# Softmax attention and output projection of a hybrid block: a written order on four engines in place of a planned one

## The chip, the core and the metric

The kernel runs on one core of a Trainium2 chip. The core has a matrix engine (TensorE, PE in the profile, with its weight loads as PEld), three engines for elementwise work (VectorE = DVE, ScalarE = ACT, GpSimd = POOL) and a queue that issues transfers (SyncE = SP). [...] The metric is the device time of one launch in microseconds. Before the change it was 778.51 us, the median of three runs (777.87 to 778.65).

## The reference

One layer of a transformer block on 512 tokens of width 1024. The normed input is projected; a gated linear attention (GLA) of four heads and a softmax attention (MLA) of eight heads run on the projection; their gated sum goes through an output projection; a squared-ReLU MLP and a final norm follow. What matters here:

```python
    def attend(qblk):
        s = jnp.einsum('bhqd,bhkd->bhqk', qblk, kt).astype(jnp.float32)
        p = jax.nn.softmax(s, axis=-1)
        return jnp.einsum('bhqk,bhkv->bhqv', p.astype(vt.dtype), vt)
...
    merged = jax.nn.sigmoid(z_ma) * y_gla + jax.nn.sigmoid(z_mb) * y_mla
    h = h + merged @ w_out[l]
    m = rmsnorm(h, g_mlp[l])
    h = h + jnp.square(jax.nn.relu(m @ w_ff1[l])) @ w_ff2[l]
```

## The kernel before

**Numbers in two halves.** [...] `split` (line 92) is the pair: ACT copies the source into the high half, then DVE (or POOL, if told) subtracts the high half from the source into the low half. So a low half always waits for its high half. A product is three matmuls, `mm3` (lines 88 to 90).

**Attention.** There are 8 heads of 4 tiles of 128 queries, 32 tiles in all. The loop behind line 1243 counts n from 0 to 37. In step n it computes the scores of tile n (`att_scores`, line 1000), transposes the probabilities of tile n-3 (`att_flip`, line 1018) and, in odd steps, multiplies two tiles with the values (`att_values`, line 1029). `att_scores` is: three matmuls into a bank `s`, the row maximum on DVE (L1007), the exponential with its row sum on ACT (L1010), the reciprocal of the sum on DVE (L1011), and the scaling of the tile by it, on DVE for odd tiles (L1013) and on ACT for even ones (L1015). `att_flip` is four transposes into a bank `tp` (L1024) and a `split` of it into `pT` (ACT at L93, DVE at L94). The banks of `s` and `tp` come out of one set of four in PSUM. After the fourth tile of a head, `merge` (line 1045) multiplies the result by its gate on DVE (L1052) and adds the GLA part on POOL (L1055).

**Units.** `up_units(pr)` (line 945) is a generator for the pair of heads pr: first loads and splits of the pair's weights (high halves on ACT, low ones on POOL), then, one piece per call, the queries (two split pairs), the keys (two) and the values (two calls, one each). They are interleaved with the steps.

**Output projection.** It is computed with seven block products in place of eight: 1, 2, 5, 6, 3, 7 and 4, each of 24 matmuls for two row blocks (`wo_product`, line 1463). Its left operands are sums of blocks of the merged rows: `split_first` gives those of products 1 and 2, `split_sum` those of 5 and 6 (from y) and of 7 and 3 (from z), where `merged_sums` makes y and z. Its right operands are the four blocks B11, B12, B21, B22 of `w_out` and sums of them. A sum comes about in one of two ways: `load_onto` (line 904) has POOL issue two transfers that add a block out of memory onto a tile, and `add_w2` (line 910) adds on DVE. `split_part` splits one half of such a tile (two 128 x 512 parts) for TensorE.

**After the projection** the rows are added to the residual (`add_rows`), squared and scaled (`normed`, line 1309: a square on ACT, one operation on DVE, a power on POOL, one scaling on DVE and one on ACT), transposed (`flipped`), and the first two products of the MLP begin.

**What sets the order.** A planner orders the instructions of each engine by the program's order, by when operands and buffers come free, and by a table of costs, at the time the program is built. `in_program_order(start, engines)` (line 110) ties each instruction traced since `start` to the one before it on its engine, so that engine runs exactly as written; `goes_behind` ties one group behind another. Before the change, everything on ACT and DVE up to the third GLA head and the whole projection on PE, ACT and DVE run as written, attention on POOL alone; on PE, ACT and DVE the planner orders attention. SP is always the planner's.

Of the kernel before, what the change touches and what calls it, by code (L numbers as in the profile page):

```python
# [15 lines left out]
ALU = mybir.AluOpType  # L16
# [3 lines left out]
S = 512  # L20
# [36 lines left out]
def tile_block(ctx: ExitStack, tc: tile.TileContext, t, out: bass.AP):  # L57
# [16 lines left out]
    def sm(name, n=4, dt=F32):  # L74
        return tl([P, n], dt, "sm", 24, name)
# [31 lines left out]
    def traced():  # L107
        return len(nc.cur_bb.bb.instructions)
# [755 lines left out]
    def split_first(left, px, name, rest=nc.vector, g=None, c=slice(0, S)):  # L864

        g = u4(f"ga{name}") if g is None else g
        split(g[:, 0, c], g[:, 1, c], px[:, c], rest)
        left[1] = g[:, 0, 0:HT], g[:, 1, 0:HT]
        left[2] = g[:, 0, HT:S], g[:, 1, HT:S]
        return g  # L870

    def split_sum(left, src, m_lo, m_hi, name, rest=nc.vector):
        h, l = u2(f"gh{name}", F32R), u2(f"gl{name}", F32R)
        split(h, l, src, rest)
        left[m_lo] = h[:, 0:HT], l[:, 0:HT]
        left[m_hi] = h[:, HT:S], l[:, HT:S]
# [17 lines left out]
    def block_rows(w, qd, x, g, pp_):  # L894
        r = (qd * FQ + 2 * (2 * g + pp_) + x // 2) * P
        c = (x % 2) * S
        return w[r : r + P, c : c + S]

    def load_w2(qd, x, w=w2):
        for g, dst in enumerate(block_tiles(x)):  # L900
            for pp_ in range(2):
                nc.sync.dma_start(dst[:, pp_, :], block_rows(w, qd, x, g, pp_))

    def load_onto(dst, x, w):

# [4 lines left out]
    def add_w2(dst, x, y, op):  # L910
        for g in range(NP // 2):
            nc.vector.tensor_tensor(wq[dst][g], wq[x][g], wq[y][g], op=op)  # L912

    def split_part(x, g, name):
        wh, wl = halves(2, S, f"{name}{g}")
# [3 lines left out]
    def split_w2(x, name):  # L919
        return [split_part(x, g, name) for g in range(NP // 2)]  # L920
# [77 lines left out]
    probs, pTs, avs = {}, {}, {}  # L998

    def att_scores(head, qt):  # L1000
        q, kb, _, _ = heads[head]
        tok = slice(qt * P, (qt + 1) * P)
        acc = ps("at", f"s{head}{qt}")
        d = slice(0, NOPE + ROPE)
        mm3(acc, q[d, 0, tok], q[d, 1, tok], kb[d, 0, :], kb[d, 1, :], True, True)
        top = sm("top", 1)
        nc.vector.tensor_reduce(top, acc, axis=AX.X, op=ALU.max, negate=True)  # L1007
        e = u2(f"e{head}{qt}")
        tot = sm("tot", 1)
        nc.scalar.activation(e, acc, AF.Exp, bias=top, accum_out=tot)  # L1010
        nc.vector.reciprocal(tot, tot)  # L1011
        if qt % 2:
            nc.vector.tensor_scalar(e, e, tot, None, op0=ALU.mult)  # L1013
        else:
            nc.scalar.activation(e, e, AF.Copy, scale=tot)  # L1015
        probs[head, qt] = e

    def att_flip(head, qt):
        e = probs.pop((head, qt))
# [219 lines left out]
    rs = gla_squares(h, os)  # L1239
    gla_gated(h, os, rs)  # L1240
    LAG_B, LAG_C = 3, 6
    units = iter(())
    attending = traced()
    sums_of = {}
    for n in range(4 * MH + LAG_C):
        if n % 8 == 1 and n // 8 + 1 < MH // 2:
            units = up_units(n // 8 + 1)
        scored = traced()
        if n < 4 * MH:
            att_scores(n // 4, n % 4)  # L1250
        scored = scored, traced()
        next(units, None)
        b = n - LAG_B
        if 0 <= b < 4 * MH:
            flips = traced()
            att_flip(b // 4, b % 4)
            if b == 0:
                gla_turn(GH - 1, (flips, traced()))

        ready = traced()  # L1260
        if n in (17, 25, 31):
            p = (n - 13) // 8
            y, z = sums_of.pop(p)
            split_sum(wo_left[p], y, 5, 6, f"bo{p}", nc.gpsimd)
            split_sum(wo_left[p], z, 7, 3, f"co{p}", nc.gpsimd)
            if p == 1:
                for p in range(2):
                    split_first(wo_left[p], merged[p][0], f"o{p}", nc.gpsimd)
            goes_behind((ready, traced()), scored, SPLITTERS[:1])
        if n == 20:  # L1270
# [12 lines left out]
        if c >= 0 and c % 2 == 1:  # L1283
            att_values(c // 4, (c % 4) // 2)
        if c > 0 and c % 8 == 7 and c // 8 < NP - 1:
            sums_of[c // 8] = merged_sums(c // 8, nc.gpsimd)

    hrow = []
    for i in range(NT):
# [16 lines left out]

    span = {}

    def normed(i, last_half):
        at = traced()  # L1310
        m = ms_rows[i]
        square_half(hrow[i], last_half, hparts[i], m, False)
        rs = row_rstd(hparts[i])
        nc.vector.tensor_scalar(m[:, 0:S], hrow[i][:, 0:S], rs, None, op0=ALU.mult)
        nc.scalar.activation(m[:, S:D], hrow[i][:, S:D], AF.Copy, scale=rs)
        span["norm", i] = at, traced()

    def flipped(i):
        fm.rows(i, ms_rows[i])
# [134 lines left out]

    begun = traced()
    xs_ = [ps("at", f"wox{rb}") for rb in range(2)]
    zs_ = [ps("at", f"woz{rb}") for rb in range(2)]
    ws_ = [ps("mm", f"wow{rb}") for rb in range(2)]  # L1460
# [10 lines left out]
                    m in (1, 2, 5) and p == 0, p == NP - 1, m not in (1, 2, 5))  # L1471

    last = NP - 1
    split_first(wo_left[2], merged[2][0], "o2", nc.vector)
# [4 lines left out]
    y, z = merged_sums(last, nc.vector)  # L1479
    split_sum(wo_left[last], y, 5, 6, f"bo{last}")  # L1480
    wo_right[5].append(split_part(B11, 1, "bo5"))
    load_onto(B12, B22, w_out)
    add_w2(B11, B22, B11, ALU.add)
    for rb in range(2):
        add_rows(rb, 0, xs_[rb])
    wo_product(2)
    wo_right[6] = [split_part(B11, 0, "bo6")]
    for rb in range(2):
        add_rows(rb, 0, ws_[rb])
        first_half_square(rb, 0)  # L1490
    wo_right[6].append(split_part(B11, 1, "bo6"))
    load_onto(B11, B21, w_out)
    load_w2(0, B21)
    split_sum(wo_left[last], z, 7, 3, f"co{last}")
    wo_product(5)
    wo_right[3] = [split_part(B22, 0, "bo3")]
    for rb in range(2):
# [20 lines left out]
    for rb in range(2):  # L1518
        wo_product(7, (rb,))
        add_rows(2 + rb, 1, xs_[rb], ALU.subtract)  # L1520
        first_half_square(2 + rb, 1)
        flipped(rb)
    early.append(proj_begin(w1, P, "f01", "at"))
    for rb in range(2):
        wo_product(4, (rb,))
        add_rows(2 + rb, 0, xs_[rb])
        normed(2 + rb, 0)
    proj_run(early[0], mT, 0)
    proj_run(early[1], mT, 0, range(5))
    flipped(2)  # L1530
# [80 lines left out]
```

## Time and profile before

| | us |
|---|---|
| median of three runs | 778.51 |
| the profiled execution | 777.01 |
| its span, first to last instruction | 775.3 |
| TensorE busy | 757.8 |
| VectorE busy | 584.6 |
| ScalarE busy | 452.9 |
| GpSimd busy | 148.9 |
| first scores of attention begin | 303.73 |
| first product of the projection begins | 388.0 |

A row of a view begins with its start in us where it is a timeline, then the length, the engine, the line of the kernel, the operation and what it writes from what. In brackets is the idle time of the engine just before it, with the instruction whose end ended that idle time. A row of groups has the number of instructions behind an x, then their busy time in us and the mean of one in ns, then the idle time ahead of them.

### The profile page before, as it was taken

The page shows a single profiled execution, that of the slowest core. Times are in us where ns is not written, and L with a number is a line of the kernel's source. Part 1 is how long each engine was busy: PE and PEld are TensorE (multiplying, and loading weights), DVE is VectorE, ACT ScalarE, POOL GpSimd, SP SyncE. Part 2 cuts the span into 40 slices and gives each one's busy share as a digit, 9 for nine tenths or more (in the row PEclk, how much of TensorE's full clock was granted, in tenths as well). Part 3 has the DMA queues.
Part 4 walks back from the last instruction along what each step waited for, and adds up shares of the span by engine and source line. Part 5 has one row for each costly group of instructions (what it writes and reads, how often), then busy time and mean ns, then how long its engine had stood idle before and what let it go on. Part 6 is the DMA issues. An engine that isn't in the chain of part 4 may idle for free.

```text
span 775.3 us, 10210 instructions
## 1 busy us (share of the span) xinstructions
PE 757.8 (98%) x3744; PEld 640.1 (83%) x3744; DVE 584.6 (75%) x866; ACT 452.9 (58%) x768; POOL 148.9 (19%) x224
## 2 busy tenths in 40 slices
PE   9999999999999999999799899999999999999996
PEld 7888788889888888898687788888888888888885
DVE  7788999666677776989887677965787578848695
ACT  7556667556475546978735675544644465336644
POOL 0810006161533124044741000000000000000014
PEclk9999999999999999999899899999999999999999
DMA  9734201132325324014766231164106510560002
GB/s 313 244 110 135 71 18 29 54 82 55 82 55 135 52 55 106 22 36 142 219 162 187 84 109 55 58 202 120 55 30 188 151 40 27 171 183 0 28 1 108
DMA packets 94945, 77.09 MB, mean 99 GB/s; under 512 B 15312, under 2 KB 74704, under 8 KB 94896
## 3 DMA queue, kind: packets, MB, share of 16 engines
q1 hardware_dynamic: 92752, 72.24, 31.6%
q0 software_dynamic: 1856, 3.93, 2.7%
q8 instruction: 29, 0.48, 0.3%
q10 hardware_dynamic: 288, 0.28, 0.1%
q14 instruction: 20, 0.16, 0.1%
HBM read 72.76 MB, written 2.10 MB: 97 GB/s over the span
## 4 chain that ended last, share of the span: by engine, by line
PE 93%; DVE 4%; issue 1%; ACT 1%; POOL 0%; POOLq 0%; DVEq 0%; ACTq 0%
PE f L89 8%; PE f L90 8%; PE f L88 8%; PE gx L88 4%; PE gx L89 4%; PE gx L90 4%; PE first L326 3%; PE za L88 2%; PE za L89 2%; PE za L90 2%; PE gz L89 2%; PE gz L90 2%; PE gz L88 2%; PE tp L1024 2%; PE zb L88 1%; PE zb L90 1%
## 5 line engine op out<-in xcount | busy, mean ns | idle before, releaser
L1550 POOL DMA_DIRECT2D gfin<-in_g_final x1 | 0.6, 622 | 283.7 <-PE f L90 283.7
L912 DVE TENSOR_TENSOR w<-w,w 128x1024 f32<-128x1024 f32 x34 | 41.1, 1220 | 0.3
L474 POOL COPY v3f<-rrf 128x4 f32<-128x4 f32 x4 | 2.8, 708 | 135.8 <-DVE rrf L457 135.8
L1010 ACT ACTIVATE e<-s,top 128x512 f32<-128x512 f32 x32 | 21.9, 685 | 6.7 <-DVE top L1007 6.1
L1298 DVE TENSOR_TENSOR h<-h,gx 128x512 f32<-128x512 f32 x32 | 21.5, 680 | 1.9 <-PE gx L90 1.8
L1007 DVE TENSOR_REDUCE top<-s 128x1 f32<-128x512 f32 x32 | 21.6, 679 | 1.4 <-PE s L90 1.4
L94 DVE TENSOR_TENSOR pT<-tp,pT 128x512 fp32r<-128x512 f32 x32 | 21.5, 679 | 0.4 <-ACT pT L93 0.2
L93 ACT ACTIVATE pT<-tp 128x512 fp32r<-128x512 f32 x32 | 18.8, 594 | 4.9 <-PE tp L1024 4.9
L88 PE MATMUL av<-pT,v 128*128 128x256 f32 x64 | 19.5, 304 | 1.3 <-ACT pT L93 1.3
L1024 PE MATMUL tp<-ident,e 128*128 128x128 f32 x128 | 20.1, 281 | 0.0
L89 PE MATMUL av<-pT,v 128*128 128x256 f32 x64 | 18.6, 291 | 0.1
L1024 PEld LDWEIGHTS tp<-ident,e 128*128 128x128 f32 x128 | 16.2, 146 | 3.1 <-issue 0.4
L1370 ACT ACTIVATE fa<-f 128x512 f32<-128x512 f32 x32 | 18.5, 577 | 0.0
L90 PE MATMUL av<-pT,v 128*128 128x256 f32 x64 | 18.4, 288 | 0.0
L93 ACT ACTIVATE ghb<-y 128x512 fp32r<-128x512 f32 x16 | 10.1, 632 | 14.0 <-DVE y L859 14.0
L94 DVE TENSOR_TENSOR sc<-sc,sc 128x512 fp32r<-128x512 f32 x16 | 10.9, 690 | 9.5 <-ACT sc L93 9.5
L88 PE MATMUL s<-kbuf,q 96*128 96x512 f32 x32 | 14.5, 453 | 3.2 <-DVE pT L94 3.2
L93 ACT ACTIVATE sc<-sc 128x512 fp32r<-128x512 f32 x16 | 9.3, 596 | 11.5 <-DVE sc L545 11.5
L1055 POOL TENSOR_TENSOR mx<-tb,za 128x256 f32<-128x256 f32 x8 | 6.9, 868 | 40.9 <-DVE tb L1052 40.9
L93 ACT ACTIVATE b_00h<-w 128x1024 fp32r<-128x1024 f32 x7 | 7.4, 1060 | 12.6 <-PE gx L90 6.0
L93 ACT ACTIVATE b_10h<-w 128x1024 fp32r<-128x1024 f32 x7 | 7.4, 1061 | 12.1 <-PE gz L90 6.0
L93 ACT ACTIVATE b_20h<-w 128x1024 fp32r<-128x1024 f32 x7 | 7.4, 1060 | 11.9 <-PE gz L90 6.0
(1639 smaller groups left out, 2940.7 us busy)
## 6 DMA issues: line engine op xcount, KB each, us to landing
w<-in_w_ff SPq DMA_DIRECT2D x64, 256.0 KB, 3.4
grw<-in_w_in SPq DMA_DIRECT2D x8, 512.0 KB, 8.6
gvw<-in_w_in SPq DMA_DIRECT2D x8, 512.0 KB, 4.8
w<-in_w_out SPq DMA_DIRECT2D x16, 256.0 KB, 5.2
w<-in_w_out POOLq DMA_DIRECT2D x6, 512.0 KB, 7.9
x<-in_xt SPq DMA_DIRECT2D x8, 256.0 KB, 5.3
vw<-in_w_first SPq DMA_DIRECT2D x8, 256.0 KB, 5.4
h<-in_x SPq DMA_DIRECT2D x4, 512.0 KB, 10.7
```

The costliest lines, as they stand in the source:

```text
L88: nc.tensor.matmul(acc, lh, rh, start=start, stop=False, skip_group_check=onto)
L89: nc.tensor.matmul(acc, lh, rl, start=False, stop=False, skip_group_check=onto)
L90: nc.tensor.matmul(acc, ll, rh, start=False, stop=stop, skip_group_check=onto)
L93: nc.scalar.activation(hi, src, AF.Copy)
L94: rest.tensor_tensor(lo, src, raw(hi), op=ALU.subtract)
L326: nc.tensor.matmul(f_accs[i], a[:, i * P : (i + 1) * P], b, start=k == 0 and x == 0, stop=k == KD - 1 and x == 2)
L912: nc.vector.tensor_tensor(wq[dst][g], wq[x][g], wq[y][g], op=op)
L1007: nc.vector.tensor_reduce(top, acc, axis=AX.X, op=ALU.max, negate=True)
L1010: nc.scalar.activation(e, acc, AF.Exp, bias=top, accum_out=tot)
L1024: nc.tensor.transpose(tp[:, k * P : (k + 1) * P], e[:, k * P : (k + 1) * P], ident)
L1298: nc.vector.tensor_tensor(hc, hc, acc, op=op)
L1370: nc.scalar.activation(a, acc, AF.Relu)
```

## The change

- All of PE, ACT, DVE and POOL run as written from the loop's begin (`attending`) to the end of the projection. The `goes_behind` calls of the loop go.
- The reciprocal and the scalings leave `att_scores`. `att_normalise`, at the begin of each even step, takes one reciprocal for tiles n-2 and n-1 together and scales the first on ACT and the second on DVE.
- The units of pair 1 begin ahead of the loop, those of pairs 2 and 3 load in steps 6 and 14; the pieces come in steps with n % 8 from 2 to 6.
- The weights of products 1 and 2 no longer pass through the tiles of B11 and B21: `streamed` loads each half into a staging buffer and splits it in steps 11, 13, 21 and 23. Tile B21 is then filled with block B22, and POOL's transfers add B11 and B12 onto it (steps 27 and 31): the weights of product 6, which DVE added before. B21 itself is added onto it for product 4.
- Sums and splits of the left operands get steps of their own; one `split_first` goes from POOL to DVE.
- In the projection `normed` is taken apart into `second_half_square` and `scaled`, the latter with both halves on ACT for the first two row blocks, and the order of the pieces around products 3, 7 and 4 is another.

```diff
-    def load_w2(qd, x, w=w2):
+    def load_w2(qd, x, w=w2, block=None):
...
+    def streamed(m, x, g):
+
+        wf = stage(2, S, f"bo{m}{g}")
+        for pp_ in range(2):
+            nc.sync.dma_start(wf[:, pp_, :], block_rows(w_out, 0, x, g, pp_))
+        wh, wl = halves(2, S, f"bo{m}{g}")
+        split(wh, wl, wf)
+        wo_right.setdefault(m, []).append((wh, wl))
...
-        tot = sm("tot", 1)
-        nc.scalar.activation(e, acc, AF.Exp, bias=top, accum_out=tot)
+        if qt % 2 == 0:
+            tots[head] = sm("tot", 2)
+        tot = tots[head]
+        nc.scalar.activation(e, acc, AF.Exp, bias=top, accum_out=tot[:, qt % 2 : qt % 2 + 1])
+        probs[head, qt] = e
+
+    def att_normalise(head, qt):
+        tot, a, b = tots[head], probs[head, qt], probs[head, qt + 1]
         nc.vector.reciprocal(tot, tot)
-        if qt % 2:
-            nc.vector.tensor_scalar(e, e, tot, None, op0=ALU.mult)
-        else:
-            nc.scalar.activation(e, e, AF.Copy, scale=tot)
-        probs[head, qt] = e
+        nc.scalar.activation(a, a, AF.Copy, scale=tot[:, 0:1])
+        nc.vector.tensor_scalar(b, b, tot[:, 1:2], None, op0=ALU.mult)
...
-    units = iter(())
+    units = up_units(1)
+    next(units)
     attending = traced()
     sums_of = {}
     for n in range(4 * MH + LAG_C):
-        if n % 8 == 1 and n // 8 + 1 < MH // 2:
-            units = up_units(n // 8 + 1)
-        scored = traced()
+        if n % 2 == 0 and 2 <= n <= 4 * MH:
+            att_normalise((n - 2) // 4, (n - 2) % 4)
         if n < 4 * MH:
             att_scores(n // 4, n % 4)
-        scored = scored, traced()
-        next(units, None)
+        if 2 <= n % 8 < 7:
+            next(units, None)
+        if n in (6, 14):
+            units = up_units(n // 8 + 2)
+            next(units)
...
-        ready = traced()
-        if n in (17, 25, 31):
...
+        for x, at in (("y", (18, 26, 32)), ("z", (20, 28, 33))):
+            if n in at:
+                p = at.index(n)
+                to = (5, 6) if x == "y" else (7, 3)
+                split_sum(wo_left[p], sums_of[p, x], *to, f"{x}o{p}", nc.gpsimd)
+        if n in (19, 30):
+            p = (19, 30).index(n)
+            split_first(wo_left[p], merged[p][0], f"o{p}", nc.gpsimd)
+        if n == 35:
+            split_first(wo_left[2], merged[2][0], "o2")
+        if n in (11, 13):
+            streamed(1, B11, (n - 11) // 2)
+        if n in (21, 23):
+            streamed(2, B21, (n - 21) // 2)
+        if n == 22:
             load_w2(0, B11, w_out)
-            load_w2(0, B21, w_out)
-        if n == 24:
-            wo_right[1] = split_w2(B11, "bo1")
+        if n == 23:
+            load_w2(0, B21, w_out, B22)
+        if n == 25:
+            load_onto(B11, B12, w_out)
         if n == 27:
-            wo_right[2] = split_w2(B21, "bo2")
+            load_onto(B21, B11, w_out)
         if n == 28:
-            load_onto(B11, B12, w_out)
-        if n == 30:
             load_w2(0, B12, w_out)
             load_w2(0, B22, w_out)
+        if n == 31:
+            load_onto(B21, B12, w_out)
+        if n == 34:
+            load_onto(B12, B22, w_out)
...
-    load_onto(B12, B22, w_out)
-    add_w2(B11, B22, B11, ALU.add)
+    load_w2(0, B11)
...
-    wo_right[6] = [split_part(B11, 0, "bo6")]
+    wo_right[6] = [split_part(B21, 0, "bo6")]
...
-        normed(rb, 1)
-        wo_right.setdefault(4, []).append(split_part(B11, rb, "bo4"))
-    load_w2(0, B11)
+        second_half_square(rb, 1)
+    wo_right[4] = [split_part(B21, 0, "bo4")]
+    for rb in range(2):
+        scaled(rb, True)
+    wo_right[4].append(split_part(B21, 1, "bo4"))
+    load_w2(0, B21)
+    wo_product(7, (0,))
+    add_rows(2, 1, xs_[0], ALU.subtract)
+    first_half_square(2, 1)
+    flipped(0)
+    wo_product(7, (1,))
+    add_rows(3, 1, xs_[1], ALU.subtract)
+    first_half_square(3, 1)
     early = [proj_begin(w1, 0, "f00", "at")]
...
-    in_program_order(begun, PE_ONLY + SPLITTERS)
-    in_program_order(attending, (mybir.EngineType.Pool,))
+    in_program_order(attending, PE_ONLY + SPLITTERS + (mybir.EngineType.Pool,))
```

More of the change, by code (lines that the diff above doesn't have):

```diff
@@ L1486, in tile_block @@
     wo_product(2)
-    wo_right[6] = [split_part(B11, 0, "bo6")]
+    wo_right[6] = [split_part(B21, 0, "bo6")]
     for rb in range(2):
         add_rows(rb, 0, ws_[rb])
+    wo_right[6].append(split_part(B21, 1, "bo6"))
+    load_onto(B21, B21, w_out)
+    split_sum(wo_left[last], z, 7, 3, f"co{last}")
+    for rb in range(2):
         first_half_square(rb, 0)
[L1491 to L1494, printed above, removed]
     wo_product(5)
@@ L1513, in tile_block @@
         add_rows(rb, 1, zs_[rb])
-        normed(rb, 1)
-        wo_right.setdefault(4, []).append(split_part(B11, rb, "bo4"))
-    load_w2(0, B11)
-    early = [proj_begin(w1, 0, "f00", "at")]
[L1518 to L1522, printed above, removed]
+        second_half_square(rb, 1)
+    wo_right[4] = [split_part(B21, 0, "bo4")]
+    for rb in range(2):
+        scaled(rb, True)
[8 more added lines that the diff above has]
+    first_half_square(3, 1)
+    early = [proj_begin(w1, 0, "f00", "at")]
+    flipped(1)
     early.append(proj_begin(w1, P, "f01", "at"))
@@ L1525, in tile_block @@
         wo_product(4, (rb,))
+        at = traced()
         add_rows(2 + rb, 0, xs_[rb])
-        normed(2 + rb, 0)
+        second_half_square(2 + rb, 0)
+        scaled(2 + rb, False)
+        span["norm", 2 + rb] = at, traced()
     proj_run(early[0], mT, 0)
```

29 lines of the change are left out of this document (10 added, 19 removed).

## The prediction

> **What bounds the kernel now.** I read the page first, then the busy times of the engines in three stretches: the attention loop up to its last weight loads, its end, and the output projection.
>
> ```profile
> PE 757.8 (98%) x3744; PEld 640.1 (83%) x3744; DVE 584.6 (75%) x866; ACT 452.9 (58%) x768; POOL 148.9 (19%) x224
> 303.73:359.00 55.27, 55.27 (x367) 49.67 (x366) 49.44 (x101) 46.10 (x104) 15.52 (x21) 1.00 0.27 77
> 359.00:388.00 29.00, 24.45 (x154) 21.49 (x153) 26.26 (x45) 22.42 (x47) 21.33 (x21) 0.88 0.51 150
> 388.00:445.00 57.00, 52.62 (x268) 44.23 (x267) 40.92 (x64) 29.39 (x54) 13.12 (x18) 0.94 0.56 146
> ```
>
> The columns of a stretch are its length, then the busy time of PE, PEld, DVE, ACT and POOL, the granted clock, and two of DMA. TensorE is busy in 98% of the span, and in the first 55 us of attention without a gap. There is something to win only where it is not: 29.00 - 24.45 = 4.6 us in the end of attention and 57.00 - 52.62 = 4.4 us in the projection. The order in time on TensorE shows where, and two short stretches show what follows a gap.
>
> ```profile
> 372.51 0.38 PE L88 MATMUL av<-pT,v 128*128 128x256 f32 x1 [1.35 <-ACT pT L93]
> 375.62 0.79 PE L88 MATMUL s<-kbuf,q 96*128 96x512 f32 x1 [2.73 <-DVE pT L94]
> 430.64 0.79 PE L88 MATMUL wox<-bo40h,gdo 128*128 128x512 f32 x1 [3.08 <-DVE h L1298]
> 375.00:380.00 5.00, 4.38 (x14) 3.58 (x15) 3.60 (x8) 2.65 (x6) 5.00 (x6) 0.50 0.89 290
> 430.00:435.00 5.00, 4.36 (x10) 3.47 (x11) 3.83 (x9) 4.38 (x13) 0.37 (x2) 0.50 0.64 206
> ```
>
> After each of the two long gaps the granted clock is 0.50 in the next stretch, so about 4.4 us of work takes twice its time: another 2.2 us each. All that a perfect order of these stages could win is therefore 4.6 + 4.4 + 2.2 + 2.2 = 13.4 us.
>
> **The change, part by part.** It fixes the order of ACT, DVE, PE and POOL from the first attention step to the projection's end as it is written. In step n the writing gives, on DVE: (reciprocal and one scaling, n even), the maximum of tile n, a unit's low halves, the low half of the transposed tile n-3. On ACT: (one scaling, n even), the exponential of tile n, a unit's high halves, the high half of tile n-3. The queues take turns: the exponential waits for the maximum; the high half stands behind the exponential; the low half waits for the high half; and the next maximum stands behind the low half. That is a ring through two engines, once per step, and TensorE cannot shorten it. Its durations:
>
> ```profile
> L1007 DVE TENSOR_REDUCE top<-s 128x1 f32<-128x512 f32 x32 | 21.6, 679 | 1.4 <-PE s L90 1.4
> L94 DVE TENSOR_TENSOR pT<-tp,pT 128x512 fp32r<-128x512 f32 x29 | 19.6, 678 | 0.4 <-ACT pT L93 0.2
> L1013 DVE TENSOR_SCALAR e<-e,tot 128x512 f32<-128x512 f32 x16 | 9.9, 620 | 0.4
> L1011 DVE RECIPROCAL tot<-tot 128x1 f32<-128x1 f32 x32 | 4.9, 155 | 2.6 <-ACT e L1010 2.5
> L1052 DVE SCALAR_TENSOR_TENSOR tb<-tb,av 128x512 f32<-128x512 f32 x7 | 4.8, 680 | 1.2 <-PE av L90 1.2
> L94 DVE TENSOR_TENSOR bo10l<-w,bo10h 128x1024 fp32r<-128x1024 f32 x1 | 1.2, 1220 | 0.0
> L1010 ACT ACTIVATE e<-s,top 128x512 f32<-128x512 f32 x32 | 21.9, 685 | 6.7 <-DVE top L1007 6.1 <-DVE tot L1011 0.4
> L1015 ACT ACTIVATE e<-e,tot 128x512 f32<-128x512 f32 x16 | 11.5, 717 | 0.3 <-DVE tot L1011 0.3
> L93 ACT ACTIVATE pT<-tp 128x512 fp32r<-128x512 f32 x30 | 17.7, 593 | 4.9 <-PE tp L1024 4.9
> L93 ACT ACTIVATE bo10h<-w 128x1024 fp32r<-128x1024 f32 x1 | 1.0, 1048 | 0.0
> L93 ACT ACTIVATE wk2h<-wk2f 128x128 fp32r<-128x128 f32 (+1 forms) x4 | 1.1, 351 | 0.0
> L93 ACT ACTIVATE wq3h<-wq3f 128x384 fp32r<-128x384 f32 x1 | 0.5, 519 | 0.0
> 366.64 0.68 DVE L1007 TENSOR_REDUCE top<-s 128x1 f32<-128x512 f32 x1
> 367.35 0.69 ACT L1010 ACTIVATE e<-s,top 128x512 f32<-128x512 f32 x1 [0.25 <-DVE top L1007]
> 367.94 0.19 ACT L1010 ACTIVATION_READ_ACCUMULATOR e<-s,top 128x1 f32 x1
> 368.03 0.59 ACT L93 ACTIVATE pT<-tp 128x512 fp32r<-128x512 f32 x1
> 383.08 0.68 DVE L1007 TENSOR_REDUCE top<-s 128x1 f32<-128x512 f32 x1
> 383.68 0.68 DVE L94 TENSOR_TENSOR pT<-tp,pT 128x512 fp32r<-128x512 f32 x1
> 384.28 0.68 DVE L1007 TENSOR_REDUCE top<-s 128x1 f32<-128x512 f32 x1
> 383.01 0.60 ACT L93 ACTIVATE pT<-tp 128x512 fp32r<-128x512 f32 x1 [0.41 <-PE tp L1024]
> 383.86 0.69 ACT L1010 ACTIVATE e<-s,top 128x512 f32<-128x512 f32 x1 [0.25 <-DVE top L1007]
> ```
>
> From maximum to exponential is 367.35 - 366.64 = 0.71; from there to a high half on the same engine 368.03 - 367.35 = 0.68; the high half lasts 0.59, and a waiting engine starts about 0.03 later, as the exponential did (366.64 + 0.68 = 367.32): 0.62; on DVE one operation follows another after 0.60 (383.08, 383.68, 384.28). Sum 2.61 us a step. The rows at 383 show how the kernel before avoids it: there ACT does the high half (383.01) ahead of the exponential (383.86), so DVE goes maximum, low half, maximum in 1.2 us.
>
> That a written order really turns in such rings, the attention's predecessor shows, which already runs in written order: masked copy and low half on DVE, high half on ACT.
>
> ```profile
> 179.51 0.60 ACT L93 ACTIVATE sc<-sc 128x512 fp32r<-128x512 f32 x1 [0.96 <-DVE sc L545]
> 181.07 0.60 ACT L93 ACTIVATE sc<-sc 128x512 fp32r<-128x512 f32 x1 [0.96 <-DVE sc L545]
> 180.14 0.69 DVE L94 TENSOR_TENSOR sc<-sc,sc 128x512 fp32r<-128x512 f32 x1 [0.66 <-ACT sc L93]
> 180.74 0.29 DVE L545 COPY_PREDICATED sc<-after,bds 128x128 f32<-128x128 int32 x1
> ```
>
> One turn takes 181.07 - 179.51 = 1.56; by my rule 0.63 + 0.60 + 0.29 + 0.03 = 1.55. The ring is counted rightly to a hundredth. [...]
>
> Now the terms, for steps 3 to 31 (29 steps):
> - The ring alone: 29 x 2.61 = 75.7.
> - In the 14 even steps DVE does the shared reciprocal (0.155 + 0.03) and one scaling (0.40 at its usual pace) ahead of the maximum: 14 x 0.59 = 8.3. ACT's scaling (0.72) runs beside DVE's and the maximum and costs nothing; without that cover it is 14 x 0.6 = 8.6. Sharing the reciprocal saves 16 x 0.155 = 2.5 of DVE time, already in this.
> - Units. A low half in the ring adds 0.60 for each of v's two. For q and k two pairs read one bank, and the trace has the second high half waiting for the first low half:
>
> ```profile
> 352.61 0.68 DVE L94 TENSOR_TENSOR kbuf<-uk,kbuf 64x512 fp32r<-64x512 f32 x1
> 353.32 0.59 ACT L93 ACTIVATE kbuf<-uk 64x512 fp32r<-64x512 f32 x1 [0.51 <-DVE kbuf L94]
> ```
>
>   So 0.71 + 0.62 + 0.60 = 1.93 more each, or 1.2 if q does not wait so. In steps 3 to 31: k three times, q twice, v six times: 5 x 1.93 + 6 x 0.60 = 13.3 (9.6 at the least).
> - The next pair's weights (steps 6 and 14): ACT's high halves stand between exponential and high half, 1.1 + 0.5 less the overlap, about 1.4 each: 2.8.
> - Two gates turned (step 3) and six merges, 0.60 each on DVE: 4.8.
> - The four streamed weight parts (11, 13, 21, 23): ACT's 1.05 starts 0.48 after the high half (which follows as ACT's operations do), DVE's 1.22 behind it starts at 1.56 and frees DVE at 2.70 where it was free at 1.22: 4 x 1.5 = 5.9. At the least DVE's own 4 x 1.13 = 4.5.
>
> Sum 75.7 + 8.3 + 13.3 + 2.8 + 4.8 + 5.9 = 110.8 us.
>
> ```profile
> 306.46 1.87 DVE L1007 TENSOR_REDUCE top<-s 128x1 f32<-128x512 f32 x3
> 386.98 0.68 DVE L94 TENSOR_TENSOR pT<-tp,pT 128x512 fp32r<-128x512 f32 x1
> 400.74 2.36 DVE L912 TENSOR_TENSOR w<-w,w 128x1024 f32<-128x1024 f32 x2
> L908 POOL DMA_DIRECT2D w<-in_w_out x6 | 7.4, 1373 | 1.0 <-DVE bo61l L94 1.0
> ```
>
> The first maxima stand at 306.46 now and should after; two exponentials, the reciprocal, the third maximum and q's pairs bring the maximum of tile 3 to about 313.1, so the low half of tile 28 (step 31) ends near 313.1 + 110.8 = 423.9. Now it is at 386.98 + 0.60 = 387.6. **The loop costs +36.3 us.** The three low halves, two value products and the merges behind it are the same work as now: 0, within 2.
>
> The projection: the weight sum on DVE (2.36) goes, but DVE is not what TensorE waits for there except at 430: 0, at best -2.4 were it on the path. Two sums more by transfers are four issues more on POOL (1.37 each, 5.5 us) and eight more loads on SP; POOL is busy 21 of 29 us at the end of attention now, and with 36 us more to do it in, nothing waits for it; without that cover up to 5.5. The stall at 430 is late rows: now an addition stands behind normalising and two weight splits. After, it stands behind four ACT scalings (4 x 0.72 = 2.9) and the second part of the weights of product 4, while TensorE has one block (2.8) to do: much the same gap. I take -1; the bounds are -6.6 (gap and clock gone) and +3 (both scalings fully in the open).
>
> Against the profiled execution, 777.01 us (span 775.3 and 1.7 around it): 777.0 + 36.3 - 1 = 812.3. It lies 1.5 below the median of the runs, 778.51, so for the median **814 us**.
>
> **The rivals.**
> *The written order fits, faster.* The two gaps go and the ring does not bind, because ACT or DVE are never late: 778.5 - 13.4 = 765 at best. For it: both engines have idle time in each step (49.4 and 46.1 busy of 55.3). Against it: attention up to the last low half takes 387.6 - 306.46 = 81 us now, and the ring with nothing but its even steps takes 32 x 2.61 + 15 x 0.59 = 92. It decides from a ring under 81 / 32 = 2.5 us.
> *Only the bare ring, little slower.* Units, streams and merges slip into DVE's waiting time instead of adding to it: 92 - 81 = +11, less 1: 789. For it: DVE waits 1.4 of every 2.6 us. Against it: in the queue the additions stand behind ACT work that itself follows the exponential, past that wait.
> *The clock falls, much slower.* TensorE has 55.27 + 24.45 = 79.7 us of work, 2.2 of it an effect of the half clock, in some 121 us, with a gap in nearly every step. If those gaps held the clock at 0.50, it would need 2 x 77.5 = 155 where stage and gaps take 84 now: +71, 849. For it: the clock fell after the gaps of 4.1 and 3.1 us. Against it: gaps here are about 1 us each. [...]
> *The order isn't followed.* If the added order edges did not bind ACT and DVE, their planner would be as free as now, only the moved weights and sums would count: between 765 and 779.
>
> **How the numbers follow.** Full ring 0.76; bare ring 0.08; half clock 0.04; written order fits 0.09; order not followed 0.03. The full ring's own range: at the least 36.3 - 3.7 - 1.4 - 2 - 6.6 = +22.6, so 801; at the most DVE's scaling at twice its pace while POOL works (14 x 0.5 = 7), 3 in the projection instead of -1, 5.5 of POOL, 2 in the tail and two falls of the clock (2 x 2.2): +36.3 + 22, so 837. To leave no more than 2 in 10 out, the range goes down to the bare ring: 788 to 837. No change can be told within 0.2%, about 1.6 us. Slower: 0.76 + 0.08 + 0.04 = 0.88; of the two others 0.02 falls within 0.2%, and 0.10 is faster.
>
> **What would show it.** In the profile after: ACT's idle time ahead of the exponential put down to the maximum rises from 6.1 us to some 30; DVE's ahead of the low half, put down to ACT, from 0.2 to over 15; TensorE's busy share in the attention near 0.7; maxima 2.6 us apart in odd steps without a unit and 3.2 in even ones. I am wrong if maxima of steps 24 to 31 come at less than 2.5 us apart on average, if ACT does a high half ahead of the exponential of its step, or if the clock in attention is not near 1.

## The result, and the profile after

| | before | after |
|---|---|---|
| median of four runs, us | 778.19 (777.27 to 778.65) | 823.56 (823.01 to 824.18) |
| ratio to before, 95% interval | | 1.0585 (1.0566 to 1.0603) |
| the profiled execution, us | 777.01 | 823.11 |
| its span, us | 775.3 | 821.4 |

The change costs 45 us. The kernel before has one run more here than in the table ahead of the prediction, 777.27, so its median is 778.19 in place of 778.51. Of the page after, the busy times first:

```profile
PE 773.0 (94%) x3744; PEld 648.2 (79%) x3744; DVE 581.8 (71%) x846; ACT 457.5 (56%) x770; POOL 151.2 (18%) x228
```

DVE and ACT do as much as before (584.6 and 452.9 us); the span has grown by 46.1 us, TensorE's busy time by 15.2, with the same 3744 matmuls. So nothing was added to be done: TensorE waits, and part of its work runs slower. The busy times in three stretches of the kernel after, columns as in the prediction (length, PE, PEld, DVE, ACT, POOL, clock, DMA):

```profile
303.73:359.00 55.27, 43.84 (x234) 36.05 (x232) 33.75 (x59) 30.80 (x65) 4.93 (x8) 0.88 0.11 28
359.00:428.00 69.00, 48.16 (x267) 40.02 (x267) 41.28 (x68) 38.75 (x83) 31.42 (x37) 0.88 0.56 161
428.00:485.00 57.00, 51.80 (x258) 44.43 (x259) 35.82 (x57) 29.88 (x54) 15.89 (x19) 0.94 0.58 139
```

In the first 55 us of attention TensorE had no gap before (busy 55.27 of 55.27); now it is idle for 55.27 - 43.84 = 11.4, and for 20.8 in the next 69. No engine is full in either stretch. Who waits for whom stands in the groups of instructions of the kernel after (its L1022 is the exponential, L1017 the maximum, L1028 ACT's scaling, L1027 the shared reciprocal, L1037 the transposes):

```profile
L1037 PE MATMUL tp<-ident,e 128*128 128x128 f32 x128 | 23.8, 317 | 27.5 <-ACT e L1028 25.6
L94 DVE TENSOR_TENSOR pT<-tp,pT 128x512 fp32r<-128x512 f32 x32 | 22.0, 689 | 29.4 <-ACT pT L93 29.3
L1022 ACT ACTIVATE e<-s,top 128x512 f32<-128x512 f32 x32 | 22.0, 687 | 30.2 <-DVE top L1017 30.2
L1028 ACT ACTIVATE e<-e,tot 128x512 f32<-128x512 f32 x16 | 11.6, 722 | 20.3 <-DVE tot L1027 20.3
```

DVE waits 29.3 us for ACT's high half ahead of its low half (0.2 before), ACT waits 30.2 for DVE's maximum ahead of its exponential (6.1 before). Two engines that wait 30 us for each other, neither of them full: that is the ring. The chain of waits in order of time shows two turns of it, each piece with its start, its length and what ran:

```profile
416.93 0.60 DVE top L1017
417.56 0.78 ACT e L1022 x2
418.34 0.49 ACT pT L93
418.85 0.69 DVE pT L94
419.54 0.61 DVE top L1017
420.18 0.78 ACT e L1022 x2
420.96 0.49 ACT pT L93
421.47 0.69 DVE pT L94
```

No TensorE piece is in it. From low half to low half one turn takes 421.47 - 418.85 = 2.62 us.

### The profile page after: what moved, and what is told of

The parts are those of the page before. It is cut to its first block, busy times and chain, and to the rows that moved or that the text cites. A ratio compares the mean times of both kernels' runs of the same rounds, so it can differ in the third digit from the quotient of the medians.

```text
span 821.4 us, 10236 instructions
## 1 busy us (share of the span) xinstructions
PE 773.0 (94%) x3744; PEld 648.2 (79%) x3744; DVE 581.8 (71%) x846; ACT 457.5 (56%) x770; POOL 151.2 (18%) x228
## 4 chain that ended last, share of the span: by engine, by line
PE 79%; DVE 10%; ACT 7%; issue 2%; POOL 1%; DMA 0%; POOLq 0%; ACTq 0%; DVEq 0%
PE f L89 7%; PE f L90 7%; PE f L88 7%; PE gx L88 4%; PE gx L89 4%; PE gx L90 4%; PE first L326 3%; ACT e L1022 3%; DVE top L1017 2%; DVE pT L94 2%; PE za L88 2%; PE za L89 2%; PE za L90 2%; PE gz L89 2%; PE gz L88 2%
## 5 line engine op out<-in xcount | busy, mean ns | idle before, releaser
L1037 PE MATMUL tp<-ident,e 128*128 128x128 f32 x128 | 23.8, 317 | 27.5 <-ACT e L1028 25.6
L1037 PEld LDWEIGHTS tp<-ident,e 128*128 128x128 f32 x128 | 17.3, 162 | 36.3 <-ACT e L1028 30.7
L94 DVE TENSOR_TENSOR pT<-tp,pT 128x512 fp32r<-128x512 f32 x32 | 22.0, 689 | 29.4 <-ACT pT L93 29.3
L913 DVE TENSOR_TENSOR w<-w,w 128x1024 f32<-128x1024 f32 x32 | 38.7, 1219 | 0.3
L1022 ACT ACTIVATE e<-s,top 128x512 f32<-128x512 f32 x32 | 22.0, 687 | 30.2 <-DVE top L1017 30.2
L88 PE MATMUL av<-pT,v 128*128 128x256 f32 x64 | 23.0, 359 | 0.6 <-DVE tb L1065 0.6
L1028 ACT ACTIVATE e<-e,tot 128x512 f32<-128x512 f32 x16 | 11.6, 722 | 20.3 <-DVE tot L1027 20.3
L1017 DVE TENSOR_REDUCE top<-s 128x1 f32<-128x512 f32 x32 | 21.7, 680 | 0.0
L89 PE MATMUL av<-pT,v 128*128 128x256 f32 x64 | 21.5, 335 | 0.0
L90 PE MATMUL av<-pT,v 128*128 128x256 f32 x64 | 21.4, 335 | 0.0
L88 PEld LDWEIGHTS av<-pT,v 128*128 128x128 f32 x64 | 15.6, 244 | 0.8 <-issue 0.8
L90 PEld LDWEIGHTS av<-pT,v 128*128 128x128 f32 x64 | 15.7, 246 | 0.0
```

The costliest lines, as they stand in the source:

```text
L88: nc.tensor.matmul(acc, lh, rh, start=start, stop=False, skip_group_check=onto)
L89: nc.tensor.matmul(acc, lh, rl, start=False, stop=False, skip_group_check=onto)
L90: nc.tensor.matmul(acc, ll, rh, start=False, stop=stop, skip_group_check=onto)
L94: rest.tensor_tensor(lo, src, raw(hi), op=ALU.subtract)
L1037: nc.tensor.transpose(tp[:, k * P : (k + 1) * P], e[:, k * P : (k + 1) * P], ident)
```

## The experiments

Each "ratio" is to the kernel before, run on the same chip at the same time, with its 95% interval. Medians are of four runs.

**The exponential behind the high half.** The kernel after, with one ACT instruction elsewhere: in step n the exponential of tile n follows the high half of tile n-3. All four engines still run as written. What `att_scores` did behind the maximum becomes `att_exp`, which `att_flip` calls through `between`.

```diff
         nc.vector.tensor_reduce(top, acc, axis=AX.X, op=ALU.max, negate=True)
+        scored_[head, qt] = acc, top
+
+    def att_exp(head, qt):
+        acc, top = scored_.pop((head, qt))
         e = u2(f"e{head}{qt}")
...
+        nc.scalar.activation(hi[:, :, c], src, AF.Copy)
+        between()
+        nc.vector.tensor_tensor(lo[:, :, c], src, raw(hi[:, :, c]), op=ALU.subtract)
...
+            att_flip(b // 4, b % 4, (lambda: att_exp(n // 4, n % 4)) if n < 4 * MH else (lambda: None))
```

> The changed kernel with one thing moved: on ACT the exponential of tile n stands behind the high half of tile n-3 instead of ahead of it. DVE, PE and POOL keep their written order. Ring theory: the ring max, exp, high half, low half then runs over two steps (about 1.3 us a step), so TensorE bounds the loop again with its 80 us: 768 to 790 us, and ACT's idle time ahead of the exponential falls from 30 us to under 12. Rival (TensorE's written order, or the moved weights and added transfers, cost the time): 812 to 824 us, hardly changed.

Measured: 790.3 us (789.21 to 791.23), ratio 1.0163 (1.0145 to 1.0181). Some 33 of the 45 us are gone with this one move. The groups of this kernel (its lines are five further down):

```profile
L1027 ACT ACTIVATE e<-s,top 128x512 f32<-128x512 f32 x32 | 22.0, 689 | 4.8 <-DVE top L1018 4.7
L1033 ACT ACTIVATE e<-e,tot 128x512 f32<-128x512 f32 x16 | 11.6, 723 | 12.3 <-DVE tot L1032 12.3
```

ACT's wait for the maximum falls from 30.2 to 4.7 us, as the ring says; the time lies 0.3 us above the expected range. What is left is a wait of ACT's scaling for the shared reciprocal, 12.3 us.

**The written order alone.** The kernel before, with nothing of the change but the order of PE, ACT and DVE; it has a reciprocal for each tile.

```diff
-    in_program_order(begun, PE_ONLY + SPLITTERS)
-    in_program_order(attending, (mybir.EngineType.Pool,))
+    in_program_order(attending, PE_ONLY + SPLITTERS + (mybir.EngineType.Pool,))
```

> The kernel before with nothing but the written order on PE, ACT and DVE in attention; no moved weights, no shared reciprocal. Ring theory: the same ring, with the reciprocal inside it (even tiles 0.71 + 0.90 + 0.61 + 0.62 + 0.60 = 3.4 us, odd ones 2.6, on average 3.0 against 2.9 in the changed kernel, and units and splits on top): 812 to 835 us. Rival (the moved weights, sums and transfers carry the loss): 776 to 792 us.

Measured: 826.0 us (825.32 to 826.61), ratio 1.0623 (1.0607 to 1.0639). In its groups ACT waits even longer for the maximum:

```profile
L1010 ACT ACTIVATE e<-s,top 128x512 f32<-128x512 f32 x32 | 22.0, 687 | 47.7 <-DVE top L1007 47.7
```

**All but the written order.** The kernel after, with the planner given back PE, ACT and DVE in attention.

```diff
+    begun = traced()
     xs_ = [ps("at", f"wox{rb}") for rb in range(2)]
...
-    in_program_order(attending, PE_ONLY + SPLITTERS + (mybir.EngineType.Pool,))
+    in_program_order(begun, PE_ONLY + SPLITTERS)
+    in_program_order(attending, (mybir.EngineType.Pool,))
```

> The changed kernel with PE, ACT and DVE left to the planner in the attention loop, as they are in the kernel before; the shared reciprocal, the streamed weights, the sums by transfers and the projection's new order stay. Ring theory: 768 to 788 us. Rival (moved weights and added transfers): 810 to 824 us.

Measured: 780.6 us (780.13 to 780.7), ratio 1.0038 (1.0023 to 1.0052). With the run above that settles where the loss lies: the order alone costs 6.2%, all the rest 0.4%, both together 5.85%. This kernel's own small loss is in its waits (who waits for whom: idle time in all, times, longest):

```profile
POOL w L909 <- DMA w<-in_w_out: 6.6, 2, 3.8
PE wox L88 <- ACT gao L93: 6.2, 1, 6.2
```

POOL, which still runs as written, has the issue of a weight sum (L909) ahead of the last head's additions. Two such issues wait 6.6 us in all for transfers that come before theirs; the additions stand behind it, and TensorE waits 6.2 us for the rows that come of them at the begin of the projection.

**ACT and DVE given to the planner, PE and POOL as written.**

```diff
-    in_program_order(attending, PE_ONLY + SPLITTERS + (mybir.EngineType.Pool,))
+    in_program_order(begun, SPLITTERS)
+    in_program_order(attending, PE_ONLY + (mybir.EngineType.Pool,))
```

> The changed kernel with ACT and DVE left to the planner in the attention loop; PE and POOL stay as written there, and the projection stays as written on all. Ring theory: the ring is gone wherever the planner takes high halves ahead of exponentials: 768 to 795 us. Rival (PE's written order or the moved weights): 812 to 824 us.

Measured: 782.0 us (780.68 to 783.56), ratio 1.0051 (1.0032 to 1.007). That is within 1.4 us of the run before it, which differs only in that the planner has PE too: the written order of PE costs next to nothing more. (POOL runs as written in both, and in the kernel before.) The loss sits in the order of ACT and DVE.

**A reciprocal for each tile, in the kernel after.** TensorE's largest wait above, 25.6 us, is for the scaling of even tiles (L1028), which waits for the reciprocal of two. Is that a cause of its own, or a place where the ring shows?

```diff
         nc.vector.reciprocal(tot, tot)
-        nc.scalar.activation(a, a, AF.Copy, scale=tot[:, 0:1])
-        nc.vector.tensor_scalar(b, b, tot[:, 1:2], None, op0=ALU.mult)
+        if qt % 2:
+            nc.vector.tensor_scalar(e, e, tot, None, op0=ALU.mult)
+        else:
+            nc.scalar.activation(e, e, AF.Copy, scale=tot)
...
-        if n % 2 == 0 and 2 <= n <= 4 * MH:
-            att_normalise((n - 2) // 4, (n - 2) % 4)
+        if 1 <= n <= 4 * MH:
+            att_normalise((n - 1) // 4, (n - 1) % 4)
```

> The changed kernel, ring and order kept, with a reciprocal for each tile. Ring theory: 17 reciprocals more at 0.19 us in the ring (+3), and in the tail tile 30 no longer waits for tile 31 (-4 to -6): 818 to 824 us. Rival, TensorE's 25.6 us of waiting for the scaling of even tiles is a cause of its own and not a form of the ring: under 805 us.

Measured: 825.65 us (825.25 to 826.1), ratio 1.0615 (1.0595 to 1.0635). That is 1.7 us above the range of the ring theory, which had counted on 4 to 6 us less at the end of the loop, and 20 above the rival. The waits of this kernel (L1020 is the exponential, L1029 ACT's scaling) show the time moved, not gone:

```profile
ACT e L1020 <- DVE top L1017: 42.0, 16, 3.6
PE s L88 <- ACT e L1020: 13.8, 15, 1.7
PE tp L1037 <- ACT e L1029: 1.4, 1, 1.4
```

TensorE's wait for the scaling falls from 25.6 to 1.4 us, and 13.8 us of waiting for the exponential stand in its place, where there were 4.4. So TensorE's 25.6 us were the ring seen from another side: a loop that turns too slowly lets its consumer wait at whichever place comes last.

**The same with the exponential behind the high half.** With the first ring gone, the wait left over is the shared reciprocal; here each tile gets its own.

> The kernel with the exponential behind the high half (790.3 us), and a reciprocal for each tile by itself at the begin of the step after its exponential. If the pairing is what is left (TensorE waits 9.2 us for the scaling of even tiles there, with two falls of the clock behind the longest waits): 776 to 783 us. Rival, the waits only move: 788 to 792 us.

Measured: 803.65 us (802.01 to 804.03), ratio 1.0325 (1.03 to 1.035). The expectation failed by 20 us and with the wrong sign. Its timeline (start, length, engine, line) shows what is new:

```profile
402.92 0.68 DVE L1018 TENSOR_REDUCE top<-s 128x1 f32<-128x512 f32 x1
403.70 0.69 ACT L1025 ACTIVATE e<-s,top 128x512 f32<-128x512 f32 x1 [1.94 <-DVE top L1018]
404.51 0.16 DVE L1030 RECIPROCAL tot<-tot 128x1 f32<-128x1 f32 x1 [0.31 <-ACT e L1025]
404.59 0.67 DVE L1018 TENSOR_REDUCE top<-s 128x1 f32<-128x512 f32 x1
```

The maximum of tile n stands on DVE behind the reciprocal of tile n-1, which waits for the exponential of n-1, which waited for the maximum of n-1. That is a second ring through the same two engines; a reciprocal for each tile turns it every step, the shared one every second step. By itself it isn't long: 404.59 - 402.92 = 1.67 us. What bounds the later half of this kernel's attention is a longer way round, over two steps, as three rows of its chain of waits show:

```profile
395.70 0.69 DVE pT L1048
399.50 0.61 ACT e L1034
400.63 0.69 DVE pT L1048
```

From one low half the chain goes over DVE's scaling and maximum to ACT's exponential, then over ACT's scaling of that same tile and a high half to the low half two steps on: 400.63 - 395.70 = 4.93 us. ACT's scaling can stand there, one step behind its exponential, because the tile has its own reciprocal. That this accounts for all of the 13 us over the shared reciprocal isn't shown. The pairing, which I had taken for the cause of a wait, was rather a cure. The same run has a gap near the end of attention:

```profile
409.89 1.20 POOL L909 DMA_DIRECT2D w<-in_w_out  x1 [0.94 <-DMA w<-in_w_out]
410.45 5.07 DVE L94 TENSOR_TENSOR gao<-mx,gao 128x512 fp32r<-128x512 f32 x1
415.44 0.41 DVE L1073 SCALAR_TENSOR_TENSOR tb<-tb,av 128x256 f32<-128x256 f32 x1
415.99 0.55 PE L88 MATMUL av<-pT,v 128*128 128x256 f32 x1 [5.64 <-DVE tb L1073]
```

TensorE's last value product waits 5.64 us for the merge on DVE (L1073), which stands behind a low half of 128 x 512 that takes 5.07 us beside POOL's work; and POOL's work comes at that moment because an issue ahead of it waited for a transfer. The next run puts the two last weight sums behind the loop:

```diff
-        if n == 31:
-            load_onto(B21, B12, w_out)
-        if n == 34:
-            load_onto(B12, B22, w_out)
...
+    load_onto(B21, B12, w_out)
+    load_onto(B12, B22, w_out)
     hrow = []
```

> The same, and POOL's last two weight sums (onto B21 and B12) issued behind the merges of the last head. If POOL's wait for earlier transfers holds up those merges here too: 3 to 8 us under the one with a reciprocal per tile, 770 to 778 us. Rival, POOL is not late in this order: the same within 1 us.

Measured: 798.1 us (797.66 to 799.51), ratio 1.0264 (1.0243 to 1.0284): 5.6 us less, inside the expected 3 to 8; the 770 to 778 rested on the expectation that had just failed. The gap ahead of that value product is 1.24 us. The second ring stays.

**The late sums with the exponential behind the high half, reciprocals shared.**

> The kernel with the exponential behind the high half (790.3 us, reciprocals shared), and POOL's last two weight sums behind the merges of the last head. If the 12 us that it still lies above the kernel before are partly POOL's lateness at the projection's begin, as the 5.6 us between the two kernels with a reciprocal per tile say: 783 to 787 us. Rival, all of it is waiting for the shared reciprocal: 789 to 791 us.

Measured: 789.5 us (789.17 to 790.14), ratio 1.0159 (1.0141 to 1.0177), no better than without the late sums, as the rival said. The expected 5 us weren't there to be had: here TensorE waits 9.2 us, in 8 places, for the scaling behind the shared reciprocal, just as without them:

```profile
PE tp L1042 <- ACT e L1033: 9.2, 8, 2.7
```
So the early sums in POOL's queue cost only where what stands behind them is what TensorE waits for last.

**The late sums with the planner.** All but the written order, and the two sums behind the loop.

> The kernel with all of the change but the order (780.6 us), and the last two weight sums behind the merges. It has a gap of 6.2 us at the projection's begin, where POOL waited 6.6 us for transfers ahead of the merges; with the fall of the clock behind it that is some 8 us. If the added sums by transfers cause it: 769 to 775 us, under the kernel before. Rival: the merges wait for something else, 779 to 782 us.

Measured: 772.2 us (771.39 to 773.35), ratio 0.9929 (0.9907 to 0.995): 8 us better than with the early sums, and 0.7% faster than the kernel before. One gap was left in its TensorE timeline, ahead of the transposes of the scaled rows, and the last edit takes ACT's scalings ahead of both weight splits of product 4:

```profile
419.59 0.66 PE L198 MATMUL mb<-ident,ms 128*128 128x128 f32 x4 [2.90 <-ACT ms L1338]
```

```diff
-    wo_right[4] = [split_part(B21, 0, "bo4")]
     for rb in range(2):
         scaled(rb, True)
-    wo_right[4].append(split_part(B21, 1, "bo4"))
+    wo_right[4] = [split_part(B21, g, "bo4") for g in range(2)]
```

> The planned order with late sums (772.2 us), and in the projection the rows scaled ahead of both weight splits of product 4, so the scalings start some 1.5 us earlier and TensorE's gap of 2.9 us ahead of the transposes shrinks to about 1.5: 769.5 to 771.5 us. Rival, the splits come late for product 4 in turn: 772 to 774 us.

Measured: 769.6 us (769.41 to 770.08), ratio 0.9903 (0.9886 to 0.992), the lowest time of all kernels here, though its interval overlaps that of the run before it. The gap of 2.90 us is gone; one of 0.99 stands ahead of product 4 in its place. In the 84 us from the begin of attention, TensorE is busy 82.91 of 84.27 us at full clock, against 66.21 in the same stretch of the kernel after, at 0.88:

```profile
303.73:388.00 84.27, 82.91 (x549) 73.49 (x549) 77.14 (x135) 70.91 (x154) 41.95 (x48) 1.00 0.47 126
```

**The end of the loop.** In the kernel after, TensorE waits 3.86 us for the scaling of tile 30 (see below). Here the reciprocals of the last two tiles are taken apart, so that tile 30 is scaled a step sooner.

```diff
-        if n % 2 == 0 and 2 <= n <= 4 * MH:
+        if n % 2 == 0 and 2 <= n < 4 * MH:
             att_normalise((n - 2) // 4, (n - 2) % 4)
+        if n in (4 * MH - 1, 4 * MH):
+            x = n - (4 * MH - 1)
+            e, tot = probs[MH - 1, 2 + x], tots[MH - 1][:, x : x + 1]
+            nc.vector.reciprocal(tot, tot)
+            if x:
+                nc.vector.tensor_scalar(e, e, tot, None, op0=ALU.mult)
+            else:
+                nc.scalar.activation(e, e, AF.Copy, scale=tot)
```

> The changed kernel with the last two tiles' reciprocals apart, tile 30 scaled in step 31 instead of 32, all else as written. If the tail is long because TensorE stands 3.9 us at the transpose of tile 30 and then runs at half clock: 3 to 6 us less, 817.5 to 820.5 us. Rival, the tail waits for something else: 822.5 to 824.5 us.

Measured: 824.0 us (822.68 to 824.66), ratio 1.0598 (1.0574 to 1.0622): nothing gained. The gap at tile 30 is gone, and another stands six us later, as the timeline of this kernel shows:

```profile
433.36 2.18 DVE L94 TENSOR_TENSOR gao<-mx,gao 128x512 fp32r<-128x512 f32 x1
435.46 0.41 DVE L1065 SCALAR_TENSOR_TENSOR tb<-tb,av 128x256 f32<-128x256 f32 x1
436.02 0.36 PE L88 MATMUL av<-pT,v 128*128 128x256 f32 x1 [2.61 <-DVE tb L1065]
```

DVE's low half of the third of the four pairs of heads (`gao`, moved by the change ahead of the last head's merge) now falls beside POOL's additions and takes 2.18 us, where in the kernel after, a little later, it took 0.68. The merge stands behind it, and the last value product behind the merge.

## Why the prediction came out as it did

The direction, the mechanism and the place were right: a ring DVE maximum, ACT exponential, ACT high half, DVE low half, made by the written order. 814 was forecast, 823.56 measured: +36 against +45. Term by term, in the profiled executions (the loop's end before is 387.6, product 2 began at 397.0):

```profile
313.47 0.69 DVE L1017 TENSOR_REDUCE top<-s 128x1 f32<-128x512 f32 x1
395.50 0.73 POOL L1068 TENSOR_TENSOR mx<-tb,za 128x256 f32<-128x256 f32 x1 [4.23 <-DVE tot L1027]
395.53 0.98 DVE L1029 TENSOR_SCALAR e<-e,tot 128x512 f32<-128x512 f32 x1
403.46 0.49 DVE L1029 TENSOR_SCALAR e<-e,tot 128x512 f32<-128x512 f32 x1
428.45 0.69 DVE L94 TENSOR_TENSOR pT<-tp,pT 128x512 fp32r<-128x512 f32 x1 [1.39 <-ACT pT L93]
```

```profile
352.95 0.66 PE L1037 MATMUL tp<-ident,e 128*128 128x128 f32 x4 [3.15 <-ACT e L1028]
430.09 1.11 PE L1037 MATMUL tp<-ident,e 128*128 128x128 f32 x4 [3.86 <-ACT e L1028]
433.56 1.05 PE L1037 MATMUL tp<-ident,e 128*128 128x128 f32 x4
437.10 0.36 PE L88 MATMUL av<-pT,v 128*128 128x256 f32 x1 [0.61 <-DVE tb L1065]
L88 PE MATMUL wow<-bo20h,gao x4: 389/389/389, 444.1 to 446.1; 128*128 128x512 f32 x4
```

```profile
385.73 0.36 PE L88 MATMUL av<-pT,v 128*128 128x256 f32 x1
387.12 0.60 PE L1024 MATMUL tp<-ident,e 128*128 128x128 f32 x4
```

The first fence is the timeline of DVE and POOL after; the second has four rows of TensorE's timeline after, and the first group of product 2 in the view of its bank (start of the first to start of the last); the third has two rows of TensorE's timeline before.

- *The ring's turn:* 2.61 predicted, 2.62 measured. That no ready instruction of ACT or DVE passes one that waits was an assumption of the sum; no run shows it by itself, and the turn agrees with it. *The maximum of tile 3:* 313.1 predicted, 313.47 measured.
- *The loop:* predicted to end at 423.9, measured 428.45 + 0.60 = 429.05. The sum 110.8 became 115.6. Most of the difference, 3.5 us, is DVE's scaling. I priced it at its usual pace of 0.40, and as a mishap at twice its time in all of 14 steps, though the row I had printed gave a mean of 620 ns: in the kernel before, too, 4 of 16 took 0.86 to 1.48. In the kernel after, seven of 16 took 0.92 to 1.16 where the others took 0.49: six of them right behind a merge, as at 395.53, while POOL makes its additions, and one beside a low half of POOL's. A step with q's two pairs takes 345.86 - 341.18 = 4.68 from maximum to maximum instead of 4.54; were it so for all five of q and k, that is 0.7.
- *Even steps:* those with a scaling and nothing else take 369.26 - 366.04 = 3.22 to 416.85 - 413.54 = 3.31, where I had 3.20.
- *Behind the loop:* "the same work as now: 0, within 2" is **the step that failed**. From the end of the low half of tile 28 to product 2 it was 397.0 - 387.6 = 9.4 us and is 444.1 - 429.05 = 15.1: +5.7. The work is not the same: I had counted two value products, and the written order has three behind that low half (in steps 33, 35 and 37). In the kernel before, the planner had begun the first of them at 385.73 and the transposes of tile 30 at 387.12, both ahead of the mark. In the kernel after, those two pieces run from 430.09 to 433.56, at half the clock (0.50): 3.47 of the 5.7 us. The other part is waiting and the clock, which stays at 0.50 up to 435: TensorE stands still from the mark to 430.09, another 1.04, and 0.61 ahead of the last value product. The wait at 430.09 has its own reason, which I hadn't followed either: the reciprocal of tiles 30 and 31 stands on DVE behind that same low half, the scaling of tile 30 behind the reciprocal, and TensorE, which has nothing else left to do, behind both. The run with this gap removed won nothing, since another wait of like length took its place. In the kernel before, at full clock (1.00 from 383 to 384 and from 390 to 394), such transposes take 383.86 - 383.50 = 0.36 and such a product 392.90 - 391.41 = 1.49; so about 1.6 of the 3.47 is the clock's, by estimate, and 1.9 work.
- *The projection:* -1 predicted. From product 2 to the span's end it was 775.3 - 397.0 = 378.3 and is 821.4 - 444.1 = 377.3: -1.0.
- *Together:* (429.05 - 387.6) + 5.7 - 1.0 = 46.2, where the spans differ by 46.1. That the time still lies within 788 to 837 is partly luck: the tail went past its allowance of 2 us, and the 5.5 for POOL and the 3 for the projection weren't needed.

The rivals. *The bare ring* is refuted: the maxima of tiles 24 to 31 lie 3.22 us apart on average (403.86 to 426.38), where the ring with nothing but its even steps has 2.9, and the loop's end moved by 41 us, not by 11. *The order fits* is refuted by the 30 us of mutual waiting, and by the run of the order alone. *The order isn't followed* gave 765 to 779 for the case; the run that makes it so gave 780.6, because of POOL's queue, which I had costed at nothing ("nothing waits for it"); with the two sums late it gave 772.2. Under the ring this cover did hold, as far as the profile tells: in the kernel after, POOL has no wait for a transfer. A run of the kernel after with the late sums wasn't made. *The clock falls* came true in part, and a clock not near 1 in attention was one of the three signs that I had named for being wrong: it was 0.88. The other two did not show. The clock cost less than the rival said; how much of the loop is its share, no run separates, but the ring's turn of 2.62 us has no TensorE piece in it.

Three expectations on the way fell: a reciprocal for each tile behind a later exponential (it makes the second ring), the late sums without the planner, and the end of the loop. All three took the last wait in the profile for the cause; taken away, another chain of nearly the same length showed. Two more missed their range narrowly, by 0.3 us (the exponential behind the high half) and by 1.7 (a reciprocal for each tile under the ring). Moving the exponential was the one edit of the written order that opened the chain itself.

The written order isn't shown to be bound to lose. A version of it that reaches the planner's 769.6 wasn't found: with the exponential moved, 9.2 us of waits for the shared reciprocal stay, and a reciprocal for each tile only puts 9.0 us of waits for the exponential in their place.

## What to carry to other kernels

Before two engines' instructions are fixed in an order, write for one step what each stands behind and go round: if the way leads back to its start in the next step, the sum along it is the least time of a step, however idle every engine is (2.61 us counted and 2.62 measured here, with DVE and ACT busy 41.28 and 38.75 of 69.00 us), and the cure, here, was to put the instruction that finishes an older tile ahead of the one that starts a new one. A wait of the bottleneck engine names the last link, not the loop that is too long: make the edit that opens the loop. On an engine that runs as written, an issue that waits for a transfer belongs behind the arithmetic that the bottleneck engine waits for: that took 780.6 us to 772.2 with the planner and 803.65 to 798.1 with a reciprocal for each tile, and next to nothing, 790.3 to 789.5, where TensorE's last wait was another.

## What was not expected of the hardware

**The clock fell to 0.61 where no gap was longer than 1.4 us.** These are stretches of 4 and 5 us of the kernel after, early and late in attention, and two rows of TensorE's timeline:

```profile
318.00:322.00 4.00, 2.48 (x18) 2.00 (x17) 2.63 (x7) 2.06 (x5) 0.00 (x0) 1.00 0.00 0
322.00:326.00 4.00, 2.86 (x9) 1.56 (x8) 2.67 (x5) 2.17 (x5) 0.00 (x0) 0.61 0.00 0
350.00:354.00 4.00, 1.05 (x8) 1.06 (x9) 3.01 (x5) 2.24 (x5) 0.00 (x0) 0.95 0.10 31
354.00:358.00 4.00, 4.00 (x19) 3.57 (x19) 2.14 (x4) 2.54 (x7) 0.00 (x0) 0.62 0.55 125
430.00:435.00 5.00, 4.91 (x23) 4.92 (x24) 2.07 (x3) 2.50 (x6) 4.15 (x4) 0.50 0.94 145
```

```profile
320.38 0.66 PE L1037 MATMUL tp<-ident,e 128*128 128x128 f32 x4 [1.06 <-ACT e L1028]
327.41 1.12 PE L1037 MATMUL tp<-ident,e 128*128 128x128 f32 x4 [1.05 <-ACT e L1028]
```

No gap between 317 and 327 is longer than 1.4 us, and yet the four transposes take 0.66 us at 320 and 1.12 at 327, with the clock at 0.61 between. The gap of 3.15 us ahead of 352.95 still left them at 0.66, and the clock fell only behind them, to 0.62 in the stretch from 354; the one of 3.86 ahead of 430.09 had them at 1.11 at once. In the run with the exponential behind the high half, gaps of 2.72 and 2.52 us were enough for 1.11. (And the 4.1 us that the prediction called a gap were two, of 1.35 and 2.73 us, by its own rows.) From 310 to 322 TensorE was busy 62 to 70% of each 4 us and kept the full clock, 1.00; from 322 to 326, at 72%, it had 0.61. So the longest single gap alone doesn't tell, and what share over what time does, these runs don't settle. The prediction weighed single gaps only.

**An operation of DVE beside one of POOL.** The scaling of 128 x 512 takes 0.49 us alone and 0.98 beside POOL's addition (rows at 395.5). The low half of merged rows (`gao`, two inputs) takes 0.68 in the kernel after (at 435.89), and 2.18 and 5.07 in two runs above, beside several operations of POOL that follow one another. At 395.5 POOL's addition began 0.03 ahead and ended at 396.23, and DVE's scaling ended at 396.51. The low half of 5.07 us, from 410.45 to 415.52, goes further: four elementwise operations of POOL without a pause between them, from 410.65 to 414.95, lie within it. Not every operation of DVE is longer there: the low half of a transposed tile (`pT`) takes 0.69 in the kernel after at 431.87, with a low half of POOL's from 431.12 to 432.46. What makes the others longer, these runs don't show.
